# Two hybrid layers with experts on one core: adaLN weights in pairs of chunks, small operations on other engines, stores of experts' results without an order among them

## The chip, the cores and the metric

The kernel runs on one core of one Trainium2 chip. The metric is the time of one execution on the device, in microseconds (us). Three runs of the kernel before gave a median of 2566.57 us (2566.03 to 2566.64).

## The reference

The reference computes two layers of a backbone over 256 context tokens and 512 latent tokens of width 1024, all in float32. In outline, for one layer:

```python
mod = silu(c) @ w_ada + b_ada              # six vectors of 1024 for latents, six for context
h = ln(x) * (1 + scale) + shift
z = h @ w_in                               # one projection for three groups of heads
m = concat(diff_attention(z), mlstm(z), gla(z))
x = ln(ALPHA * x + gate * (m @ w_out)) * g + b
h = ln(x) * (1 + scale2) + shift2
y = sum over a token's 2 experts of weight * (silu(h @ w1[e]) * (h @ w3[e])) @ w2[e]
x = ln(ALPHA * x + gate2 * y) * g2 + b2
```

There are 32 experts in 4 groups with a hidden width of 512; a router picks one group and two experts in it for each token.

## The kernel before, in words

All work runs in the class `Net`. Each operation goes through the helper at L224, so every row of the profile has that line, and groups are told apart by the names of their tiles (out<-in). Two things set the order. `Sched` (L131) keeps a clock for each engine and, among several generators (`Thread`), goes on with the one whose operands are ready first; a generator may yield a time before which it is not to go on. What it writes is then ordered once more by the framework, which plans each engine's queue by a timeline of its own (L2228) and puts in the waits between operations that touch the same tile or tensor. Each engine works through its queue in that order.

A run goes through: the start (0 to 65 us), the mixers of layer 0 (to about 700), its routing (to 760), its experts (to 1322), the passage to layer 1 (to 1470), the mixers of layer 1 (to 1920), routing (to 1970), experts (to 2512) and the end.

`ada` (L557) computes `mod`. `w_ada` is taken in 48 chunks of 128 columns for each layer. A load brings one chunk, `wa` (at the start in tiles borrowed from `hT`), of 128 partitions by 8 by 128. Eight matmuls in four groups of 32 PSUM partitions take the four sums side by side (each is recorded as two), ACT copies PSUM to `adar`, PE transposes it, and `turn` (L567) adds the four sums and the bias `pa` on DVE. 16 chunks run at the start; 32 of layer 0 and 16 of layer 1 are strewn over the mixers of layer 0, 32 over those of layer 1, with `ADA_GAP` (L34) as the distance between them. Two chunks are loaded ahead. `h_open` (L599) opens a layer: it makes these generators, and POOL zeroes `WA` (L623), into which two loads put small gate weights. `u_mlqk` (L819) zeroes three columns of `stg` on POOL for each of four blocks.

`route` (L1673) picks experts and makes the matrices from which `slots` (L1760) computes for each expert block ("slot", up to 128 tokens; 33 in layer 0, 34 in layer 1): `ti` (rows to gather), `di` (rows to store to) and `wt` (weights). `st_slots` (L1865) then has POOL gather `xg` by an indirect DMA. `moe` (L2094) zeroes the three `xg` tiles on DVE first, ahead of the routing.

`run_visits` (L1997) goes through the experts. For wide slots `wsplit` (L1846) splits a piece of weights, 128 by 1024, into `whi` (ACT) and `wlo` = weight - `whi` (DVE or POOL). For the first visit `lo_pool` is 4 (L1597), so that all four pieces of `w1` go to POOL. Narrow slots use the weights unsplit (`part_up`, `part_act`, `part_down`; 32 or 64 columns of PE for each part). The results `ys` are stored to `ybuf` in DRAM by an indirect DMA on POOL (L1947 and L1993). Slots of one layer write other rows of `ybuf`, but to the framework each store writes the whole tensor, so it puts a wait for the former store's landing ahead of each. `part_down` takes `ys` from the two buffers that the wide slots use as well. `final_phase` (L2124) opens the next layer, loads the layer's rows of `ybuf` (L2154) and adds two rows for each token on PE (`big<-whi` or `big<-y`).

Of the kernel before, what the change touches and what calls it, by code (L numbers as in the profile page):

```python
# [7 lines left out]
F32 = mybir.dt.float32  # L8
# [9 lines left out]
D = 1024  # L18
KD = 8
# [32 lines left out]
def host_consts():  # L52
# [12 lines left out]
    def group(g):  # L65
        state["g"] = g
        off[g] = (state["n"], 0)
# [11 lines left out]
    for d in range(2):  # L79
        a, b = (s, l) if d == 0 else (l, s)  # L80
        ms = [(s // 8 == l // 8) & (a <= b)]
        for w in (8, 16, 32):
            ms.append((s // (2 * w) == l // (2 * w)) & (a // w % 2 == 0) & (b // w % 2 == 1))
        group(f"gm{d}")
        for n, m in enumerate(ms):
            add(f"gm{d}{n}", (m & same).reshape(128, 128))
    group("ml")
    add("mh", (p // 64)[:, None] == np.arange(2)[None, :])
    add("negf", np.where(p[:, None] <= p[None, :], 0.0, NEG))
# [159 lines left out]
class Net:  # L249
# [243 lines left out]
    def par0(self, pool):  # L493

        nc, I = self.nc, self.I
        pr = pool.tile([128, 128], F32, name="prow", bufs=1)
        nc.gpsimd.memset(pr, 0.0)
        nc.sync.dma_start(pr[48:56], I["c"][0].rearrange("(b p) -> b p", p=128))
        nc.sync.dma_start(pr[56:64], I["c_ctx"].rearrange("(b p) -> b p", p=128))
        nc.sync.dma_start(pr[0:48], I["b_ada"][0].rearrange("(r p) -> r p", p=128))  # L500
        nc.sync.dma_start(pr[64:112], I["b_ada"][1].rearrange("(r p) -> r p", p=128))
        ps = self.tp.tile([128, 512], F32, name="tp")
        nc.tensor.transpose(ps[:, :128], pr, self.ident)
        self.pa = self.const.tile([128, 128], F32, name="pa")
        nc.vector.tensor_copy(self.pa, ps[:, :128])
        e = self.sm.tile([128, 16], F32, name="ce", bufs=1)
        nc.scalar.activation(e, self.pa[:, 48:64], AF.Exp, scale=-1.0)
        nc.vector.tensor_scalar_add(e, e, 1.0)
        nc.vector.reciprocal(e, e)
        self.cs = self.const.tile([128, KD, 32], F32, name="cs")  # L510
        nc.gpsimd.memset(self.cs, 0.0)
        for m in range(2):
            nc.vector.tensor_mul(self.cs[:, :, m], self.pa[:, 48 + 8 * m:56 + 8 * m], e[:, 8 * m:8 * m + 8])
# [42 lines left out]

    def ada(self, pool, work, nb, gap=0.0, free=()):  # L557

        nc, I = self.nc, self.I
        chunks = [(l, ch) for l, cs in work for ch in cs]  # L560
        ws, free = {}, list(free)

        def load(x):
            w = ws[x] = free.pop(0) if free else pool.tile([128, KD, 128], F32, name="wa")
            nc.sync.dma_start(w, I["w_ada"][x[0]].rearrange("(k p) n -> p k n", p=128)[:, :, x[1] * 128:x[1] * 128 + 128])

        def turn(x, r):  # L567
            layer, ch = x
            t = self.tp.tile([128, 512], F32, name="tp")
            nc.tensor.transpose(t[:, :128], r, self.ident)  # L570
            o = self.mods[layer][:, ch, :]
            nc.vector.tensor_reduce(o, t[:, :128].rearrange("p (g m) -> p m g", g=4)[:, 0:2], axis=AX.X, op=OP.add)
            b = 64 * layer + ch
            nc.vector.tensor_scalar(o, o, self.pa[:, b:b + 1], 1.0 if ch // 8 in (1, 4) else 0.0, op0=OP.add, op1=OP.add)
            self.sch.mark(f"ada{layer}_{ch}")

        for ch in chunks[:nb]:
            load(ch)
        pend = None
        for x, ch in enumerate(chunks):  # L580
            w = ws.pop(ch)

            yield (w, self.sch.clk["tensor"] + gap)
            ps = self.mm.tile([128, 512], F32, name="mm")
            for j in range(2):
                for g in range(4):
                    nc.tensor.matmul(ps[32 * g:32 * g + 32, :128], self.cs[:, 2 * g + j, :], w[:, 2 * g + j, :],
                                     start=j == 0, stop=j == 1)
            r = self.sm.tile([128, 128], F32, name="adar", bufs=2)
            nc.scalar.activation(r, ps[:, :128], AF.Copy)  # L590
            if x + nb < len(chunks):
                load(chunks[x + nb])
            if pend:
                turn(*pend)
            pend = (ch, r)
        yield (pend[1],)
        turn(*pend)

    def h_open(self):  # L599
# [12 lines left out]
        work = ((self.i, range(16, 48)),) + (((1, range(16)),) if self.i + 1 < self.layers else ())  # L612
        self.ta = Thread(self.ada(self.pool(self.S_h, "adap", 2, self.A), work, 2, ADA_GAP[self.i]))
# [16 lines left out]
    def start(self, st):  # L630
# [3 lines left out]
        adap = self.pool(st, "adap0", 4, self.B)  # L634
        self.gar = xp

        free = [x.bitcast(F32).rearrange("p k n -> p (k n)")[:, o:o + 1024].rearrange("p (k n) -> p k n", k=KD)
                for x in self.first for o in range(0, KD * NT, 1024)]
        xs = []

# [5 lines left out]

        for t in range(TT):
            load(t)
        ta = Thread(self.ada(adap, ((0, [x + 8 * y for x in range(8) for y in range(2)]),), 16, free=free))
        ta.step()  # L650
        for x in xs:
            mv, r = self.stats(x)
# [55 lines left out]
    def projections(self):  # L708
# [1213 lines left out]
    def st_down(self, mp, its, ws):  # L1922
# [13 lines left out]
        for it in its:  # L1936
            y = mp.tile([128, D], F32, name="ys")
            m = it.n
            for h in range(2):
# [7 lines left out]
            nc.gpsimd.indirect_dma_start(out=self.ybuf[:, :],  # L1947
                                         out_offset=bass.IndirectOffsetOnAxis(ap=it.di[:m, :1], axis=0),
                                         in_=y[:m], in_offset=None, bounds_check=2 * NT - 1, oob_is_err=False)

    def part_up(self, it, ws):

# [26 lines left out]
    def part_down(self, mp, it, ws):  # L1979
# [13 lines left out]
        nc.gpsimd.indirect_dma_start(out=self.ybuf.rearrange("r (h c) -> (r h) c", h=r),  # L1993
                                     out_offset=bass.IndirectOffsetOnAxis(ap=it.di[:, :1], axis=0),
                                     in_=y, in_offset=None, bounds_check=2 * r * NT - 1, oob_is_err=False)

    def run_visits(self, mp, visits, mid=None):  # L1997

# [20 lines left out]
        for j in range(len(visits) + 1):  # L2019
            if j < len(visits):  # L2020
# [73 lines left out]
    def moe(self):  # L2094
        tc, nc, I, i = self.tc, self.nc, self.I, self.i
        self.ereg = {}
        self.nx = 0
# [26 lines left out]
    def final_phase(self):  # L2124
# [7 lines left out]
        with ExitStack() as st:  # L2132
# [22 lines left out]
            nxt = [[load(free.pop(0), self.ybuf[rows(t, o), :]) for o in (0, NT)] + [x] for t, x in zip(tiles, xs)]  # L2155
# [76 lines left out]
```

## Time and profile before

| | |
|---|---|
| median of 3 runs | 2566.57 us |
| the profiled execution | 2560.8 us, span 2559.0 us |
| busy, share of the span | PE 86%, weight loads 63%, DVE 56%, ACT 34%, POOL 26% |
| mean granted clock of PE | 0.914 |
| moved by DMA | 583.43 MB, mean 228 GB/s |
| matmuls' and loads' instructions | 14811 each |

PE, PEld, DVE, ACT, POOL and SP are the engines (TensorE's matmuls, its weight loads, VectorE, ScalarE, GpSimd and SyncE); SP issues the plain loads, POOL the indirect ones. In a row of a timeline stand start, duration, engine, operation, out<-in with the shape, the number of joined instructions and, in brackets, the engine's idle time before it and what ended that. A stretch of idle time of an engine costs only if the end waits for it.

### The profile page before, as it was taken

The page shows a single profiled execution, that of the slowest core. Times are in us where ns is not written, and L with a number is a line of the kernel's source. Part 1 is how long each engine was busy: PE and PEld are TensorE (multiplying, and loading weights), DVE is VectorE, ACT ScalarE, POOL GpSimd, SP SyncE. Part 2 cuts the span into 40 slices and gives each one's busy share as a digit, 9 for nine tenths or more (in the row PEclk, how much of TensorE's full clock was granted, in tenths as well). Part 3 has the DMA queues.
Part 4 walks back from the last instruction along what each step waited for, and adds up shares of the span by engine and source line. Part 5 has one row for each costly group of instructions (what it writes and reads, how often), then busy time and mean ns, then how long its engine had stood idle before and what let it go on. Part 6 is the DMA issues. An engine that isn't in the chain of part 4 may idle for free. (4 is left out here: it accounts for less than half of the span.)

```text
span 2559.0 us, 39336 instructions
## 1 busy us (share of the span) xinstructions
PE 2192.1 (86%) x14811; PEld 1623.5 (63%) x14811; DVE 1428.6 (56%) x2889; ACT 876.0 (34%) x1589; POOL 661.2 (26%) x537
## 2 busy tenths in 40 slices
PE   5899999978949999999956699989895999889894
PEld 3687888867846656455523488989674667555441
DVE  4566748376886445455408466665778644344313
ACT  2633212265114344444303634112622423233311
POOL 1232322110124233333312223421113322222211
PEclk9899999989969999999986789999996989889997
DMA  9253442321258889999986453313225978999995
GB/s 246 85 150 99 135 139 84 112 62 48 91 207 329 347 316 393 390 366 394 362 324 206 141 157 100 104 34 112 58 85 206 376 313 331 399 414 405 368 395 234
DMA packets 257754, 583.43 MB, mean 228 GB/s; under 512 B 47221, under 2 KB 187621, under 8 KB 208409
## 3 DMA queue, kind: packets, MB, share of 16 engines
q1 hardware_dynamic: 245368, 559.86, 59.9%
q0 software_dynamic: 12192, 21.01, 2.3%
q8 instruction: 119, 1.95, 0.3%
q14 instruction: 75, 0.61, 0.1%
HBM read 553.02 MB, written 46.27 MB: 234 GB/s over the span
## 5 line engine op out<-in xcount | busy, mean ns | idle before, releaser
L224 PE MATMUL mm<-whi,hT 128*128 128x256 f32 (+2 forms) x2144 | 482.9, 317 | 11.2 <-ACT st L224 3.8
L224 DVE TENSOR_TENSOR wlo<-wr,whi 128x1024 fp32r<-128x1024 f32 x217 | 320.8, 1498 | 132.6 <-ACT whi L224 131.6
L224 PEld LDWEIGHTS mm<-whi,hT 128*128 128x128 f32 (+1 forms) x2144 | 363.4, 199 | 40.4 <-issue 6.3
L224 POOL TENSOR_TENSOR wlo<-wr,whi 128x1024 fp32r<-128x1024 f32 x99 | 248.3, 2512 | 522.6 <-ACT whi L224 282.4
L224 ACT ACTIVATE whi<-wr 128x1024 fp32r<-128x1024 f32 x316 | 321.5, 1053 | 164.0 <-PE mm L224 83.3
L224 PE MATMUL mm<-wlo,hT 128*128 128x256 f32 (+2 forms) x1072 | 336.3, 314 | 6.6 <-POOL wlo L224 4.5
L224 PE MATMUL big<-whi,xT 128*128 128x512 f32 (+1 forms) x800 | 264.2, 406 | 4.4 <-ACT xT L224 4.0
L224 PE MATMUL big<-wr,xT 128*32 128x512 f32 (+1 forms) x1344 | 248.6, 613 | 6.9 <-DMA wr<-in_moe_w_dram 3.9
L224 PEld LDWEIGHTS mm<-wlo,hT 128*128 128x128 f32 (+1 forms) x1072 | 212.7, 198 | 23.2 <-POOL wlo L224 8.1
L224 PEld LDWEIGHTS big<-whi,xT 128*128 128x128 f32 (+1 forms) x800 | 146.6, 187 | 44.3 <-ACT xT L224 5.7
L224 POOL DMA_INDIRECT xg<-fdram,ti x67 | 86.1, 1285 | 326.1 <-DVE ti L224 274.8
L224 PE MATMUL big<-wlo,xT 128*128 128x512 f32 (+1 forms) x400 | 162.5, 406 | 1.2 <-DVE wlo L224 1.2
L224 PEld LDWEIGHTS big<-wr,xT 128*32 128x32 f32 (+1 forms) x1344 | 69.6, 126 | 143.5 <-issue 128.1
L224 PE MATMUL mm<-wr,hT 128*32 128x256 f32 (+1 forms) x1008 | 145.5, 515 | 6.1 <-DMA wr<-in_moe_w_dram 3.2
L224 PE MATMUL tp<-cst_base,xg 32*128 32x32 f32 (+3 forms) x536 | 80.8, 288 | 61.5 <-DVE wt L224 39.5
L224 PEld LDWEIGHTS tp<-cst_base,xg 32*128 32x128 f32 (+3 forms) x536 | 70.3, 198 | 91.3 <-DVE wt L224 45.5
L224 ACT ACTIVATE xT<-tp 128x512 fp32r<-128x512 f32 (+3 forms) x92 | 49.0, 532 | 227.4 <-PE tp L224 203.2
L224 PE MATMUL mm<-hT,whi 128*128 128x512 f32 (+3 forms) x400 | 112.6, 370 | 5.0 <-ACT whi L224 4.9
L224 DVE SCALAR_TENSOR_TENSOR hT<-hT,tp 128x128 f32<-128x128 f32 (+1 forms) x84 | 29.6, 353 | 153.9 <-ACT hT L224 151.8
L224 PE MATMUL mm<-wo,mT 128*128 128x512 f32 x480 | 115.4, 397 | 0.0
L224 POOL DMA_INDIRECT ybuf<-ys,di x67 | 74.7, 1115 | 111.6 <-DVE ys L224 33.1
L224 PEld LDWEIGHTS mm<-wo,mT 128*128 128x128 f32 x480 | 88.9, 188 | 19.6
(390 smaller groups left out, 3804.9 us busy)
## 6 DMA issues: line engine op xcount, KB each, us to landing
wr<-in_moe_w_dram SPq DMA_DIRECT2D x384, 1024.0 KB
wa<-in_w_ada_dram SPq DMA_DIRECT2D x84, 512.0 KB
wr<-in_w_in_dram SPq DMA_DIRECT2D x52, 512.0 KB
hT<-in_w_ada_dram SPq DMA_DIRECT2D x12, 512.0 KB
wor<-in_w_out_dram SPq DMA_DIRECT2D x12, 512.0 KB
xmid<-px SPq DMA_DIRECT2D x10, 512.0 KB
fdram<-mT SPq DMA_DIRECT2D x10, 512.0 KB
x<-xmid SPq DMA_DIRECT2D x10, 512.0 KB
```

What stands on the lines that cost most here:

```text
L224: r = f(*a, **kw)
```

## The change

- A: `ada` takes pairs of chunks, 256 columns at a time. Two loads bring a pair, each half the rows at 256 columns. Eight matmuls of 256 columns, one `adar` of 256 columns (one buffer), two transposes and two DVE operations serve two chunks. The 1 of `1 + scale` is added to `pa` beforehand. The next pair is loaded after the matmuls of this one, and the gap between pairs is twice as long.
- B: the zeros of `WA` come by two loads. C: the columns of `stg` are zeroed on DVE.
- D: the `xg` tiles are zeroed by ACT (0 times the identity).
- E: the four `wlo` of the first visit go to DVE, with a factor `one` that is computed from the second slot's `wt`, so after the routing.
- F: stores of one layer are declared free of one another. `part_down` has `ys` buffers of its own, two or four.
- G: the loads of `ybuf` in the last phase wait for each store of the layer.

```diff
@@ par0
+        for o in (8, 32):
+            v = self.pa.rearrange("p (l c) -> p l c", l=2)[:, :, o:o + 8]
+            nc.vector.tensor_scalar_add(v, v, 1.0)
@@ ada
-        chunks = [(l, ch) for l, cs in work for ch in cs]
-            w = ws[x] = free.pop(0) if free else pool.tile([128, KD, 128], F32, name="wa")
-            nc.sync.dma_start(w, I["w_ada"][x[0]].rearrange("(k p) n -> p k n", p=128)[:, :, x[1] * 128:x[1] * 128 + 128])
+        pairs = [(l, p) for l, ps in work for p in ps]
+        tiles = [(l, p, h) for l, p in pairs for h in range(2)]
+                w = ws[x] = free.pop(0) if free else pool.tile([128, 4, 256], F32, name="wa")
+                nc.sync.dma_start(w, I["w_ada"][l].rearrange("(k p) n -> p k n", p=128)[:, 4 * h:4 * h + 4, p * 256:p * 256 + 256])
...
-            nc.tensor.transpose(t[:, :128], r, self.ident)
+            for c in range(2):
+                nc.tensor.transpose(t[:, 128 * c:128 * c + 128], r[:, 128 * c:128 * c + 128], self.ident)
...
-            nc.vector.tensor_scalar(o, o, self.pa[:, b:b + 1], 1.0 if ch // 8 in (1, 4) else 0.0, op0=OP.add, op1=OP.add)
+            nc.vector.tensor_tensor(o, o, self.pa[:, b:b + 2, None].to_broadcast([128, 2, 2]), op=OP.add)
...
-                    nc.tensor.matmul(ps[32 * g:32 * g + 32, :128], self.cs[:, 2 * g + j, :], w[:, 2 * g + j, :],
-                                     start=j == 0, stop=j == 1)
-            r = self.sm.tile([128, 128], F32, name="adar", bufs=2)
-            nc.scalar.activation(r, ps[:, :128], AF.Copy)
-            if x + nb < len(chunks):
-                load(chunks[x + nb])
+                    nc.tensor.matmul(ps[32 * g:32 * g + 32, :256], self.cs[:, 4 * h + g, :], w[h][:, g, :],
+                                     start=h == 0, stop=h == 1)
...
+            r = pool.tile([128, 256], F32, name="adar", bufs=1)
+            nc.scalar.activation(r, ps[:, :256], AF.Copy)
+            load(nb + 2 * x + 2)
@@ h_open
-        self.nc.gpsimd.memset(self.WA, 0.0)
...
+            self.nc.sync.dma_start(self.WA[16 * d:16 * d + 16, 1 - d, :], self.I["cst"][0:16, o:o + 128])
@@ u_mlqk
-                for z in (0, 257, 770):
-                    nc.gpsimd.memset(raw[:, z:z + 1], 0.0)
...
+                    for z in (0, 257, 770) if t0 == part[0][0] else ():
+                        nc.vector.tensor_scalar(raw[:, z:z + 1], ps[:, 0:1], 0.0, 0.0, op0=OP.min, op1=OP.max)
@@ wsplit
-        (nc.gpsimd if pool_lo else nc.vector).tensor_tensor(lo, src, hi.bitcast(F32), op=OP.subtract)
+        if pool_lo and self.one is not None:
+            nc.vector.scalar_tensor_tensor(lo, src, self.one, hi.bitcast(F32), op0=OP.mult, op1=OP.subtract)
+        else:
+            (nc.gpsimd if pool_lo else nc.vector).tensor_tensor(lo, src, hi.bitcast(F32), op=OP.subtract)
@@ st_slots
+            if self.nx == 1:
+                self.one = self.sm.tile([128, 1], F32, name="one", bufs=1)
+                nc.vector.tensor_scalar(self.one, it.wt, -1.0, None, op0=OP.is_gt)
@@ part_down (in st_down the store is wrapped the same way)
-        y = mp.tile([128, D], F32, name="ys")[:, 0:n]
+        y = mp.tile([128, n], F32, name=f"ys{r}", bufs=r)
...
+        self.stored(nc.gpsimd.indirect_dma_start(
...
+    def stored(self, ins):
+        for x in self.stores:
+            self.tc.declare_no_dep(ins.ins, x, reason="rows of other slots")
+        self.stores.append(ins.ins)
@@ run_visits
-                self.lo_pool = 0
+                self.lo_pool, self.one = 0, None
@@ moe
-            nc.vector.memset(x, 0.0)
+            nc.scalar.activation(x.rearrange("p (a b) -> p a b", b=128), self.ident[:, None, :].to_broadcast([128, 8, 128]),
+                                 AF.Copy, scale=0.0)
@@ final_phase
+            def loady(y, src):
+                ins = nc.sync.dma_start(y, src)
+                for x in self.stores:
+                    self.tc.add_manual_dep(ins.ins, x.name, mybir.DependencyInfo(
+                        mybir.DependencyClass.Sync, mybir.DependencyReason.DATA), reason="rows of all slots")
+                return y
```

## Rows read from the trace of the kernel before

**Rows 1.** Busy time by stretch: length, PE, PEld, DVE, ACT, POOL, clock, DMA share, GB/s

```profile
768.00:1310.00 542.00, 505.76 (x2533) 305.05 (x2531) 265.56 (x355) 221.18 (x287) 173.98 (x99) 0.96 0.94 365
1984.00:2512.00 528.00, 480.11 (x2661) 291.82 (x2659) 210.10 (x339) 155.85 (x210) 139.11 (x89) 0.94 0.94 376
15.00:35.00 20.00, 14.94 (x170) 8.14 (x170) 9.10 (x33) 2.77 (x10) 2.32 (x3) 1.00 1.21 291
```

**Rows 2.** Instructions of the tile adar (ns min/median/max), and who waited for them

```profile
L224 ACT ACTIVATE adar<-mm x96: 253/277/321, 17.0 to 1553.8; 128x128 f32<-128x128 f32 x96
...
  PEld mm L224: 22.6, 20
```

**Rows 3.** Timeline of PE: a chunk of ada, and 16 records of 256 columns

```profile
1364.87 0.65 PE L224 MATMUL mm<-wa,cs 128*32 128x128 f32 x16 [1.28 <-DMA wa<-in_w_ada_dram]
...
2507.37 1.07 PE L224 MATMUL mm<-wr,hT 128*32 128x256 f32 x16 [0.97 <-DMA wr<-in_moe_w_dram]
```

**Rows 4.** Timeline of the routing of layer 0

```profile
726.71 0.15 DVE L224 TENSOR_TENSOR eg<-eg,mn 128x4 f32<-128x4 f32 x1
...
731.66 3.90 ACT L224 ACTIVATE whi<-wr 128x1024 fp32r<-128x1024 f32 x4 [2.28 <-PE mm L224]
...
732.02 0.91 DVE L224 MEMSET xg<- 128x1024 f32 x1 [0.16 <-issue]
...
732.79 9.25 POOL L224 TENSOR_TENSOR wlo<-wr,whi 128x1024 fp32r<-128x1024 f32 x4 [0.37 <-ACT whi L224]
...
735.13 2.41 DVE L224 TENSOR_TENSOR eg<-lg,rv 128x4 f32<-128x4 f32 x2
737.50 2.26 DVE L224 SCALAR_TENSOR_TENSOR eg<-eg,cst_rt 128x4 f32<-128x4 f32 x1
737.57 0.21 ACT L224 ACTIVATE eg<-eg 128x4 f32<-128x4 f32 x1 [2.02 <-DVE eg L224]
...
739.99 2.07 DVE L224 TENSOR_TENSOR eg<-eg,mn 128x4 f32<-128x4 f32 x1
...
745.33 0.50 PE L224 MATMUL tp<-cA,cnt 128*128 128x192 f32 x1 [13.70 <-DVE rv L224]
```

**Rows 5.** Waits of PE in the expert stages of layers 0 and 1: us, times, longest

```profile
PE tp L224 <- DVE wt L224: 12.9, 7, 2.3
...
PE tp L224 <- DVE wt L224: 26.6, 10, 6.0
```

**Rows 6.** The tile ybuf: who waited for it, and its DMAs from issue to landing

```profile
  DVE di L224: 1.9, 1
...
DMA to landing us min/median/max: 2.0/7.7/10.8
```

**Rows 7.** Timeline of the end of layer 0's experts

```profile
1319.93 0.98 POOL L224 DMA_INDIRECT ybuf<-ys,di  x1 [0.46 <-issue]
...
1326.51 0.48 DVE L224 TENSOR_SCALAR ys<-mm,wt 128x256 f32<-128x256 f32 x1 [9.69 <-DMA ybuf<-ys,di]
...
1336.78 0.97 POOL L224 DMA_INDIRECT ybuf<-ys,di  x1 [2.06 <-issue]
...
1342.20 3.02 PE L224 MATMUL tp<-cst_base,mod 128*128 128x128 f32 x12 [20.55 <-issue]
```

**Rows 8.** The chain that ended last (start, us, what), and PE's row of the timeline

```profile
2512.00 6.66 DMA ybuf<-ys,di
...
2519.74 2.73 DMA ybuf<-ys,di
...
2527.24 15.46 PE L224 MATMUL big<-y,cst_base 128*128 128x512 f32 x32 [15.55 <-DMA y<-ybuf]
```

**Rows 9.** Timeline of POOL, and DMA issues of 2010 to 2030 us (KB, us to landing)

```profile
2027.06 1.19 POOL L224 DMA_INDIRECT xg<-fdram,ti  x1 [8.98 <-DVE ti L224]
2028.56 1.01 POOL L224 DMA_INDIRECT ybuf<-ys,di  x1 [0.30 <-issue]
...
ybuf<-ys,di POOLq DMA_INDIRECT x2, 8.3
```

More of the change, by code (lines that the diff above doesn't have):

```diff
@@ L86, in host_consts @@
             add(f"gm{d}{n}", (m & same).reshape(128, 128))
+    group("zero")
+    add("z128", np.zeros(128))
     group("ml")
@@ L559, in ada @@
         nc, I = self.nc, self.I
[L560 to L565 removed]
+        pairs = [(l, p) for l, ps in work for p in ps]
+        tiles = [(l, p, h) for l, p in pairs for h in range(2)]
+        ws, free, ld = {}, list(free), 0
@@ L567, in turn, with load @@
+        def load(upto):
+            nonlocal ld
+            while ld < min(upto, len(tiles)):
+                l, p, h = x = tiles[ld]
+                ld += 1
+                w = ws[x] = free.pop(0) if free else pool.tile([128, 4, 256], F32, name="wa")
+                nc.sync.dma_start(w, I["w_ada"][l].rearrange("(k p) n -> p k n", p=128)[:, 4 * h:4 * h + 4, p * 256:p * 256 + 256])
         def turn(x, r):
-            layer, ch = x
+            layer, p = x
             t = self.tp.tile([128, 512], F32, name="tp")
-            nc.tensor.transpose(t[:, :128], r, self.ident)
@@ L579, in ada @@
+            o = self.mods[layer][:, 2 * p:2 * p + 2, :]
+            nc.vector.tensor_reduce(o, t[:, :256].rearrange("p (c g m) -> p c m g", c=2, g=4)[:, :, 0:2], axis=AX.X, op=OP.add)
+            b = 64 * layer + 2 * p
+            nc.vector.tensor_tensor(o, o, self.pa[:, b:b + 2, None].to_broadcast([128, 2, 2]), op=OP.add)
+        load(nb)
         pend = None
-        for x, ch in enumerate(chunks):
-            w = ws.pop(ch)
-            yield (w, self.sch.clk["tensor"] + gap)
+        for x, (l, p) in enumerate(pairs):
+            w = [ws.pop((l, p, h)) for h in range(2)]
+            yield tuple(w) + (self.sch.clk["tensor"] + gap,)
@@ L584, in ada @@
             ps = self.mm.tile([128, 512], F32, name="mm")
-            for j in range(2):
+            for h in range(2):
                 for g in range(4):
-                    nc.tensor.matmul(ps[32 * g:32 * g + 32, :128], self.cs[:, 2 * g + j, :], w[:, 2 * g + j, :],
-                                     start=j == 0, stop=j == 1)
-            r = self.sm.tile([128, 128], F32, name="adar", bufs=2)
-            nc.scalar.activation(r, ps[:, :128], AF.Copy)
-            if x + nb < len(chunks):
-                load(chunks[x + nb])
+                    nc.tensor.matmul(ps[32 * g:32 * g + 32, :256], self.cs[:, 4 * h + g, :], w[h][:, g, :],
+                                     start=h == 0, stop=h == 1)
@@ L610, in h_open @@
         self.rc = self.pool(self.S_h, "rc", 1, self.A)
-        work = ((self.i, range(16, 48)),) + (((1, range(16)),) if self.i + 1 < self.layers else ())
-        self.ta = Thread(self.ada(self.pool(self.S_h, "adap", 2, self.A), work, 2, ADA_GAP[self.i]))
+        work = ((self.i, range(8, 24)),) + (((1, range(8)),) if self.i + 1 < self.layers else ())
+        self.ta = Thread(self.ada(self.pool(self.S_h, "adap", 2, self.A), work, 2, 2.0 * ADA_GAP[self.i]))
         self.S_g = ExitStack()
@@ L622, in h_open @@
         self.WA = T("WA", [32, 2, 128])
-        self.nc.gpsimd.memset(self.WA, 0.0)
+        o, _ = self.off["zero"]
         for d in range(2):
+            self.nc.sync.dma_start(self.WA[16 * d:16 * d + 16, 1 - d, :], self.I["cst"][0:16, o:o + 128])
             self.nc.sync.dma_start(self.WA[16 * d:16 * d + 16, d, :], self.I["gl_wa"][self.i, d])
@@ L635, in start @@
         self.gar = xp
-        free = [x.bitcast(F32).rearrange("p k n -> p (k n)")[:, o:o + 1024].rearrange("p (k n) -> p k n", k=KD)
+        free = [x.bitcast(F32).rearrange("p k n -> p (k n)")[:, o:o + 1024].rearrange("p (k n) -> p k n", k=4)
                 for x in self.first for o in range(0, KD * NT, 1024)]
@@ L648, in start @@
             load(t)
-        ta = Thread(self.ada(adap, ((0, [x + 8 * y for x in range(8) for y in range(2)]),), 16, free=free))
+        ta = Thread(self.ada(adap, ((0, [x + 4 * y for x in range(4) for y in range(2)]),), 16, free=free))
         ta.step()
@@ L1946, in st_down @@
                     nc.gpsimd.tensor_tensor(y[:m, hs], y[:m, hs], self.g2[0][:m, hs], op=OP.mult)
-            nc.gpsimd.indirect_dma_start(out=self.ybuf[:, :],
-                                         out_offset=bass.IndirectOffsetOnAxis(ap=it.di[:m, :1], axis=0),
-                                         in_=y[:m], in_offset=None, bounds_check=2 * NT - 1, oob_is_err=False)
+            self.stored(nc.gpsimd.indirect_dma_start(
+                out=self.ybuf[:, :], out_offset=bass.IndirectOffsetOnAxis(ap=it.di[:m, :1], axis=0),
+                in_=y[:m], in_offset=None, bounds_check=2 * NT - 1, oob_is_err=False))
     def part_up(self, it, ws):
@@ L1992, in part_down @@
             nc.vector.tensor_scalar(y, py[:, :n], it.wt, None, op0=OP.mult)
-        nc.gpsimd.indirect_dma_start(out=self.ybuf.rearrange("r (h c) -> (r h) c", h=r),
-                                     out_offset=bass.IndirectOffsetOnAxis(ap=it.di[:, :1], axis=0),
-                                     in_=y, in_offset=None, bounds_check=2 * r * NT - 1, oob_is_err=False)
+        self.stored(nc.gpsimd.indirect_dma_start(
+            out=self.ybuf.rearrange("r (h c) -> (r h) c", h=r),
+            out_offset=bass.IndirectOffsetOnAxis(ap=it.di[:, :1], axis=0),
+            in_=y, in_offset=None, bounds_check=2 * r * NT - 1, oob_is_err=False))
+    def stored(self, ins):
+        for x in self.stores:
+            self.tc.declare_no_dep(ins.ins, x, reason="rows of other slots")
+        self.stores.append(ins.ins)
     def run_visits(self, mp, visits, mid=None):
@@ L2096, in moe @@
         self.ereg = {}
-        self.nx = 0
+        self.nx, self.one, self.stores = 0, None, []
         rp, mp = self.rpm, self.mow
@@ L2154, in final_phase @@
             xs = [load(finx.tile([128, D], F32, name=f"x{t}"), self.xmid[rows(t), :]) for t in tiles]
-            nxt = [[load(free.pop(0), self.ybuf[rows(t, o), :]) for o in (0, NT)] + [x] for t, x in zip(tiles, xs)]
+            def loady(y, src):
[4 more added lines that the diff above has]
+                return y
+            nxt = [[loady(free.pop(0), self.ybuf[rows(t, o), :]) for o in (0, NT)] + [x] for t, x in zip(tiles, xs)]
             g2 = {} if self.g2 else {m: self.modrow(5, m, f"g2{m}") for m in ms}
```

8 lines of the change are left out of this document (1 added, 7 removed).

## Prediction, made before the change was run

> **What bounds it.** I read the busy time by stretch first, then the waits inside the stretches, then timelines around each edited line. In both expert stages (542 and 528 us of the 2559 us span) PE is busy 505.76 and 480.11 us and the DMA engines show a share of 0.94 at 365 and 376 GB/s [rows 1]: there the time belongs to PE and to the weight stream almost equally, and 36 and 48 us are left in which PE does nothing. The rest of PE's idle time lies between stages: while a routing is computed, while the last results are stored and read back, and at the start. The change works on those seams, and on PE's own work in the small matmuls of `ada`. So I price seams one by one; each lies on the path if PE's gap there ends on the edited thing.
>
> **Part A, ada in pairs.** 96 chunks become 48 pairs; the 96 copies `adar` give the count [rows 2]. One chunk's 16 matmul records of 128 columns took 0.65 us at full clock; 16 records of 256 columns took 1.07 us in the form that a pair will have [rows 3]. Two chunks are 1.30, one pair is 1.07: 0.23 us saved. 16 chunks lie in the start and wait for their loads anyway, so 40 pairs count: 40 x 0.23 = 9; I take -8.5 us, since a few run beside a wait. The 96 transposes stay. On DVE, ACT and SP (still 96 loads of 512 KB, now with rows twice as long) the edit only takes away or leaves equal. Loads of matmul weights waited 22.6 us, 20 times, for `adar` copies [rows 2]; half as many copies should take part of that away, but a pair holds a PSUM buffer for longer and the copy has one buffer: between +3 and -10, I take -3. At the start 16 chunks of 512 KB arrive at 291 GB/s [rows 1], 29 us; at the stream's rate in the expert stages (376 at a share of 0.94, so 400) they would need 21. Between 0 and -8; the rows of the loads only double, to 1 KB, so I take -3.
>
> **Parts B and C, memsets off POOL.** Small work in any case: WA is 32 partitions by 256 and a margin of `stg` one column. Two more small loads stand in SP's queue beside the gate weights, and 24 tiny operations join DVE ahead of copies that wait for the same matmuls of PE: I take 0, the cover being that PE has other matmuls to go on with; without it each costs at most one such small step on DVE, 0.16 us [rows 4], 4 us in all. What the POOL memsets do to the stores behind them is counted with F.
>
> **Parts D and E, the routing.** In layer 0 DVE zeroes `xg` three times at 0.91 us before the routing's own operations. Then POOL subtracts four pieces of `wlo` for 9.25 us, and in that time three steps of the routing on DVE on 4 columns take 2.41 (two operations), 2.26 and 2.07 us, where the same subtraction took 0.15 a little earlier [rows 4]. PE waits 13.70 us for the end of this chain [rows 4]. Removed from the chain: 3 x 0.91 with their issue gaps, 3 us, and 2.41 + 2.26 + 2.07 - 4 x 0.16 = 6.1 us, together 9. What is late next is ACT: four casts of `whi` occupy it for 3.90 us from 731.66, and the Exp that the chain needs stands behind them at 737.57 [rows 4]. Three zeroings more on ACT, at about one of these casts each (3.90/4 = 1 us), can stand ahead of it too. With Exp after casts and zeroings (731.66 + 3.9 + 3 = 738.6) it would start 1 us later than now and only what comes after it (2.26 + 2.07, less normal price) is saved: -3. With Exp first of all, the whole -9. I take the middle, -5.5, in each layer, as layer 1 shows the same four pieces and the same slow operations: -11 (-5 to -18). The four `wlo` on DVE are ordered behind the second slot's weights, so while the first gather is in flight; at no more than POOL's price they need 9.25 us [rows 4], and a transfer of POOL's queue takes 7.7 [rows 6] before PE starts on the slot: covered, or up to 1.5 us late per layer, which the middle allows for.
>
> **Part F and G in the slots.** 67 slots store in turn, each store waiting until the former one has landed: 7.7 us median, 2.0 to 10.8 [rows 6]. The wait seldom reaches PE. PE's gaps that end on a slot's `wt`, computed behind `di` whose buffer such a store frees, are 12.9 us in stage 0 and 26.6 in stage 1 [rows 5]: that is the most there is, -39.5. Against it: the issue order on POOL stays, with the next gather ahead of a ready store, and a part of the gaps has its `ys` only just finished; and where the weight stream runs at its limit, PE would only catch up with it. I take a tenth, -4 (0 to -20).
>
> **The tails.** In layer 0 the last stores are chained: POOL's store at 1319.93, a `ys` that waited 9.69 us on DVE for a store to free its buffer, the last store at 1336.78, and PE idle 20.55 us until 1342.20 [rows 7]. Its last result but for that chain is ready shortly after PE's last matmul, 20.55 us before 1342.20, so 1321.65. With one buffer more per slot and no order the last `ys` ends at 1322.5, its store goes by 1324, as three follow one another at 1 us of POOL each, and lands with the median 7.7 us at 1331 against 1339 or a little more now: -8 (-3 if landings stretch, -14 if they take 2 us). In layer 1 the last two stores are at 2512.00 with 6.66 us and 2519.74 with 2.73 us, then the reads, and PE waits 15.55 us until 2527.24 [rows 8]. The second would go at 2513.2 and land 6.66 us later at 2519.9 instead of 2522.5: -2.6 (0 to -7). Sum of tails -10.5. The Trainium skill, DMA: Bandwidth & Descriptors, section "Anatomy of one DMA — SWDGE (gpsimd) path", fits 2.0 us plus the bytes at 436 GB/s, about 2.3 for one of these stores; the trace agrees only with its quickest landing, 2.0 [rows 6], and the median of 7.7 speaks against it while loads stream. By that page the last stores would land at 1326.3 and 2515.5, and the two tails would give -20.
>
> **Sum.** -8.5 - 3 - 3 - 11 - 4 - 10.5 = -40. The profiled run took 2560.8 us, so 2520.8 for it; the median of the runs shown, 2566.57, is 5.8 above it, so 2526 for a median run.
>
> **Rivals.** (1) *DVE blocks on di.* Without the chain a store no longer holds POOL, so the schedule may put `di` of a later slot earlier on DVE, where it waits for the landing of the store that frees its buffer, with `wlo` pieces behind it and PE behind those. Price: if a third of the 67 slots waits 4 us of a 7.7 us landing, 22 x 4 = +88, less the 40 won: +48, 2615; it ends slower from about 10 such waits. Against: DVE waited only 1.9 us in all for a store with `di` [rows 6], and stores now leave earlier, not later. 0.06. (2) *The weight stream takes it back.* In stages with a DMA share of 0.94 [rows 1] an earlier first slot only means an earlier wait for weights; routing and slots (-15) vanish, and what is left is -25: 2541. For it: 365 and 376 GB/s over whole stages. Against: 0.06 of 542 and 528 us is 32 and 32 us of slack, more than is won. 0.17. (3) *The stores still go one by one.* If the queue serves one transfer at a time, the wait moves from POOL into the queue: landings stay in turn, slots and tails (-14.5) vanish: 2541. The Trainium skill, same page, section "SWDGE vs HWDGE vs iDMA", says that only one such queue is allocated. Against: a gather issued at 2027.06 and a store at 2028.56 were both in flight, and stores of that stretch landed after 8.3 us all the same [rows 9]. 0.10. (4) *Pairs starve.* A pair's two tiles are requested only when the matmuls of the pair before are done, and 1 MB must then land in one gap; PE already waited 1.28 us on `wa` for a single chunk at the layer change [rows 3]. If 10 of 40 pairs wait 1.3 us more, +13: 2539. 0.12. My own case, between 2505 and 2535, has 0.50; 0.05 is for a schedule that comes out differently enough to leave the time about where it was.
>
> **How the numbers follow.** About 0.2% (5 us) is what a measurement of this kernel can tell from no change: below 2561.4 is faster, above 2571.7 slower. Faster holds my case and rivals 2, 3 and 4 (0.89), same the 0.05, slower rival 1 (0.06). All lower bounds together are -8.5 - 10 - 8 - 18 - 20 - 21 = -86; I let the range go down to -70, 2496. At the top it takes in rivals 2 to 4 and two of them together, -40 + 15 + 13 = -12, and with the upper bound of the routing instead of the middle -6, so 2560.
>
> **What would show it.** Right: `ada` records of 128x256 form in half the number; routing steps of 0.2 us on DVE and no 2 us ones, PE's gap after the router shorter by 3 to 9; stores issued about 1 us apart in the tails with overlapping landings; layer 0's gap down from 20.55 to about 12, layer 1's from 15.55 to about 13. Wrong: DVE waits for `ybuf` of tens of us (rival 1), PE waits for `wr` growing in the expert stages by what routing won (2), the last landings in the tails still 6 us apart (3), PE waits for `wa` above 10 us (4). A shift of the whole schedule, since every instruction's place is planned anew, would show as other gaps moving in stages that the edits do not touch.

## The result, and the profile after

The changed kernel took 2508.41 us (median of 4 runs), the kernel before 2566.3 us beside it: 0.9781 of it, 95% interval 0.9766 to 0.9797, or -56 us. In the experiments (changed_again) it was 0.9806 (0.9777 to 0.9835), -50 us. Forecast were 2526 us and a range of 2496 to 2560. So the time lay in the range and the sign was right. The sum was 16 us short, and its terms were wrong in both directions. One execution of stores_only, 3188 us at a granted clock of 0.635, is left out of its ratio; its other nine took 2532 to 2555 us at 0.917 to 0.928.

I cut both profiled executions at the same events on PE: the first and last matmul of a stage. The steps of the difference (after minus before) are then: start -4.7 us; mixers of layer 0 -8.1; routing -6.0; experts of layer 0 -0.3; the tail after them +0.7; opening and mixers of layer 1 -11.5; routing -7.1; experts of layer 1 -15.6; last tail -0.3. The experts' stages of the kernel before, cut like that (first `big<-whi,xT` to the last `mm<-wr,hT`; columns as in [rows 1]):

```profile
762.12:1321.65 559.53, 520.97 (x2635) 314.42 (x2634) 269.92 (x364) 224.78 (x292) 175.45 (x107) 0.96 0.93 362
1973.25:2511.69 538.44, 490.86 (x2705) 300.81 (x2704) 216.94 (x349) 161.52 (x216) 143.09 (x91) 0.93 0.92 370
```

and of the changed kernel:

```profile
743.41:1302.67 559.26, 533.49 (x2635) 315.92 (x2634) 275.94 (x362) 224.36 (x292) 179.23 (x102) 0.96 0.94 363
1936.39:2459.24 522.85, 486.75 (x2705) 296.69 (x2704) 226.41 (x349) 160.40 (x216) 143.81 (x92) 0.96 0.95 381
```

In the first stage the length stays to 0.3 us although PE has 12.8 us less idle time (38.6 and 25.8); in the second 15.6 us go and the granted clock is 0.96 instead of 0.93. Against full clock that is 0.07 of 538 us and 0.04 of 523 us, 38 and 21 us (an estimate from these rows), which is as much as the stage got shorter. Over all profiles here the kernels with ordered stores have a granted clock of 0.93 to 0.95 in that stage, those with free stores 0.95 to 0.97; that the clock rose because waits went is not shown. The wait that the stores were to shorten, `tp` for `wt` [rows 5], is gone from both stages. What leads PE's waits in the second one now (from 1937 to 2460 us):

```profile
PE tp L226 <- ACT hs L226: 10.3, 13, 1.1
PE big L226 <- DVE wlo L226: 5.9, 5, 1.6
```

Stores still land after several us, as far as the trace has it (8 of 67 landings; 61 of 67 before), and nothing but the last sums waits for them. The tile `ybuf` after, answering to [rows 6]:

```profile
who waited for it (us, times):
  PE big L226: 22.1, 2
  PEld big L226: 17.3, 3
...
DMA to landing us min/median/max: 3.7/6.7/8.2
```

The tile `adar` after, answering to [rows 2]:

```profile
L226 ACT ACTIVATE adar<-mm x48: 362/383/419, 18.9 to 1512.9; 128x256 f32<-128x256 f32 x48
...
  PEld mm L226: 2.6, 2
```

Half as many copies, and the 22.6 us that weight loads of `mm` waited for them are 2.6. That is not all time of PE: PE's own waits for `adar` went from 13.8 to 3.2 us, and the weight loads of the transposes waited 11.9 us for it instead of 5.5. The routing of layer 0 after, answering to [rows 4] (timeline):

```profile
719.19 2.95 ACT L226 ACTIVATE xg<-cst_base 128x1024 f32<-128x1024 f32 x3 [2.28 <-PE mm L226]
...
719.61 0.23 DVE L226 TENSOR_TENSOR eg<-lg,rv 128x4 f32<-128x4 f32 x2
...
722.04 3.88 ACT L226 ACTIVATE whi<-wr 128x1024 fp32r<-128x1024 f32 x4
...
723.62 0.50 PE L226 MATMUL tp<-cA,cnt 128*128 128x192 f32 x1 [4.47 <-DVE V L226]
...
725.83 0.19 ACT L226 ACTIVATE eg<-eg 128x4 f32<-128x4 f32 x1
...
734.24 2.28 POOL L226 DMA_INDIRECT xg<-fdram,ti  x1 [14.29 <-DVE wt L226]
735.59 4.88 DVE L226 SCALAR_TENSOR_TENSOR wlo<-wr,one,whi 128x1024 fp32r<-128x1024 f32 x4
...
736.83 5.06 POOL L226 DMA_INDIRECT xg<-fdram,ti  x1 [0.31 <-issue]
```

The two operations that took 2.41 us take 0.23, and PE's wait is 4.47 instead of 13.70. But Exp stands behind three zeroings and four casts on ACT, and `wt` needs it, so 9.2 us won up to PE's 723.62 are 6.0 at the first expert matmul. PE's 723.62 itself does not need Exp, which starts 2.2 us later. The second gather's issue took 5.06 us beside the four `wlo` on DVE, but 1.01 us beside the same four in another run of this kernel (changed_again) and in routing_only, so it is no lasting price of E. The Trainium skill, SBUF — State Buffer, section "SBUF: two separate sides", states an exclusive lock between DVE operations with two inputs from SBUF and POOL operations that read SBUF, held for a whole instruction; the 2.07 to 2.41 us of [rows 4], beside POOL operations of 2.3 us each, and the 0.23 here, with none beside it, agree.

The tail after layer 0, answering to [rows 7] (timeline, then the loop's line; a q after an engine is its sequencer):

```profile
1302.74 0.48 DVE L226 TENSOR_SCALAR ys<-mm,wt 128x256 f32<-128x256 f32 x1 [2.33 <-PE mm L226]
...
1315.92 3.87 PE L226 MATMUL tp<-cst_base,mod 128*128 128x128 f32 x16 [13.25 <-issue]
...
1316.43 0.97 POOL L226 DMA_INDIRECT ybuf<-ys,di  x1 [14.77 <-issue]
...
1323.46 1.84 SPq L226 DMA_DIRECT2D whi<-ybuf  x4
...
1327.20 8.84 PE L226 MATMUL big<-whi,cst_base 128*128 128x512 f32 x16 [6.79 <-DMA whi<-ybuf]
```

```profile
L2148 POOLq COMPARE_BRANCH  x3: 37/38/54, 1301.3 to 1315.5; - x3
...
L2148 POOLq INC_SWDGE_SEM  x1: 1481/1481/1481, 1308.4 to 1308.4; - x1
L2148 ACTq COMPARE_BRANCH  x1: 37/37/37, 1315.7 to 1315.7; - x1
```

The last `ys` is ready at 1303.22, its store is issued at 1316.43. In between POOL goes through L2148, a loop over experts with more tokens than their slots hold (`moe`, at L2120 in the kernel before). It runs zero times here, and still stops every engine: POOL takes its first branch at 1301.3, and ACT, the last to leave, at 1315.7. SP's waits in that time show what the loop stands still for, transfers that are in flight (1290 to 1330 us):

```profile
SPq L2148 <- DMA ybuf<-ys,di: 5.4, 1, 5.4
SPq L2148 <- DMA x<-xmid: 4.7, 1, 4.7
```

In the kernel before the loop comes after the last store and takes 4.7 us from POOL's first branch, 1337.5 to 1342.2. Freed from its order, the last store was planned behind this loop. The loads of `ybuf`, which G ties to that store, follow 7.0 us after its issue, at 1323.46. Ahead of them SP issues fifteen other loads for the next layer, one right after another from 1315.43 to 1323.42, and the landing of this store is not in the trace; so it is not shown which of the two held the loads of `ybuf`.

### The profile page after: what moved, and what is told of

The parts are those of the page before. It is cut to its first block, busy times and chain, and to the rows that moved or that the text cites. A ratio compares the mean times of both kernels' runs of the same rounds, so it can differ in the third digit from the quotient of the medians.

```text
span 2506.5 us, 37612 instructions
## 1 busy us (share of the span) xinstructions
PE 2176.8 (87%) x14043; PEld 1584.9 (63%) x14043; DVE 1426.6 (57%) x2830; ACT 870.4 (35%) x1542; POOL 646.7 (26%) x501
## 5 line engine op out<-in xcount | busy, mean ns | idle before, releaser
L226 PEld LDWEIGHTS mm<-whi,hT 128*128 128x128 f32 (+1 forms) x2144 | 361.4, 198 | 41.7 <-issue 10.3
L226 POOL TENSOR_TENSOR wlo<-wr,whi 128x1024 fp32r<-128x1024 f32 x93 | 235.6, 2535 | 365.4 <-ACT whi L226 226.7
L226 PE MATMUL big<-wr,xT 128*32 128x512 f32 (+1 forms) x1344 | 265.3, 612 | 4.5 <-DMA wr<-in_moe_w_dram 4.5
L226 PE MATMUL mm<-wr,hT 128*32 128x256 f32 (+1 forms) x1008 | 134.7, 498 | 1.5 <-DMA wr<-in_moe_w_dram 1.5
L226 POOL DMA_INDIRECT xg<-fdram,ti x67 | 92.1, 1375 | 154.1 <-DVE ti L226 104.8
L226 PEld LDWEIGHTS big<-wlo,xT 128*128 128x128 f32 (+1 forms) x400 | 74.6, 186 | 39.4 <-DVE wlo L226 15.3
```

The source lines that it names most:

```text
L226: r = f(*a, **kw)
```

## Experiments

Each is compared with the kernel before on its own chip; us are worked out from ratios of runs there (before: 2559 to 2563). Three chips served: one for stores_only, stores_undone, routing_only and ada_only, a second for changed_again, loop_store_ordered, fewer_bytes and xg_on_pool, a third for the other four. Stage lengths come from one profiled execution each, and for stages whose code is the same they scatter by 5 us and more together with the granted clock (0.96 to 0.99 in the experts of layer 0).

**stores_only**: the kernel before with the lines of F and G. **stores_undone**, and again as **stores_ordered_again**: the changed kernel without them.

```diff
@@ stores_undone, stores_ordered_again (st_down, part_down, final_phase)
-            self.stored(nc.gpsimd.indirect_dma_start(
+            nc.gpsimd.indirect_dma_start(
...
-        y = mp.tile([128, n], F32, name=f"ys{r}", bufs=r)
+        y = mp.tile([128, D], F32, name="ys")[:, 0:n]
...
-            nxt = [[loady(free.pop(0), self.ybuf[rows(t, o), :]) for o in (0, NT)] + [x] for t, x in zip(tiles, xs)]
+            nxt = [[load(free.pop(0), self.ybuf[rows(t, o), :]) for o in (0, NT)] + [x] for t, x in zip(tiles, xs)]
```

> The kernel before with parts F and G alone (stores free of one another, part_down's own ys buffers, loads of ybuf waiting for all stores). Theory 1 (the experts' stage of layer 1 got its 15.6 us from the stores, since all of PE's 26.6 us of waits for a slot's wt went away, while in stage 0 the weight stream took the 12.9 us back): -15 us, about 2551, nearly all of it in the experts of layer 1, none of it in the two tails, where the last store again stands behind the overflow loop on POOL and PE's gap stays near 20 us. Theory 2 (stage 1 was quicker because it was planned anew and began earlier, the stores have little to do with it): 0 to -4 us, 2563 to 2566, with 20 us or more of wt waits left in stage 1.

> The changed kernel without F and G: stores ordered as before, one pair of ys buffers for all. Theory 1: loses what stores gave, 2508 + 15 = 2523 us; PE's waits for wt in stage 1 are back at 20 us or more; the tails are as long as before (PE's gap 20 us after layer 0, 15.5 after layer 1), so that these neither win nor lose. Theory 2: 2508 to 2512 us. If the tails do depend on the order of the stores, this kernel's last store stands ahead of the loop on POOL, as before.

> The changed kernel without F and G once more, beside the kernel with the loop's store in order. Theory 1 (free stores are worth some 10 us in the experts' stages, 36 us of waits for wt gone and most of it taken back, and cost 2 to 4 us in the tails where the last store fell behind the loop): 2512 to 2518 us, that is 14 to 20 us above loop_store_again. Theory 2 (free stores give nothing in the experts' stages, everything is taken back): 2500 to 2508, less than 8 above loop_store_again, and that only from the tails.

Measured: alone 0.9937 (0.9912 to 0.9962), -16 us, with experts' stages of 551.2 and 528.9 us and the last store after layer 0 again behind the loop. Undone 0.9816 (0.9782 to 0.9851) and 0.9795 (0.9775 to 0.9815), where the changed kernel has 0.9806 on another chip and 0.9781 in the first measurement. So in this change the stores give nothing that can be measured, against theory 1, which gave them 15 us both ways. Beside loop_store_again, on one chip, stores_ordered_again is 15.7 us slower (2511.51 and 2495.81), as its own theory 1 had it. The mechanism of the stores is there in any case. PE's waits with stores in order (stores_ordered_again, stages 0 and 1) and its stages:

```profile
PE tp L226 <- DVE wt L226: 12.9, 7, 2.3
...
PE tp L226 <- DVE wt L226: 23.5, 8, 6.6
```

```profile
740.28:1301.14 560.86, 521.13 (x2635) 318.28 (x2634) 270.13 (x362) 225.02 (x292) 176.94 (x101) 0.96 0.93 362
1926.30:2458.40 532.10, 488.69 (x2705) 298.96 (x2704) 219.30 (x349) 161.07 (x216) 140.58 (x92) 0.94 0.94 374
```

The stages with ordered stores took 557.4 and 560.9, 532.6 and 532.1 us. With free stores and both routing edits they took 555.8, 556.0 and 550.5, and 523.0, 529.4 and 531.3 (the changed kernel and the two runs of loop_store below). The means differ by 5 and 4.5 us: some 10 us of the 36 us of waits. Over all seven profiles with free stores and D and E the first stage took 550.5 to 561.7 us and the second 522.6 to 531.3 (fewer_bytes left aside), so ordered stores lie outside the scatter only in the second, and there by little. The tail after layer 0 took 20.1 and 19.0 us with ordered stores and 22.5 and 24.5 in the changed kernel: 4 us given back. The mixers of layer 1 took 518.7 and 523.9 us in the changed kernel and 509.2 and 513.4 with ordered stores, which takes back the rest. This is not the stores' doing: xg_on_pool and fewer_bytes (below) have free stores and their last store behind the loop as well, and took 513.9 and 514.1; ada_only took 514.2. PE's sequence of operations in that stretch, told by the names of the tiles, is alike to 99% in these kernels and that of loop_store_ordered, and only to 96% between them and the changed kernel. The changed kernel alone got another plan there, 5 to 15 us longer.

**loop_store_ordered**, and again as **loop_store_again**: only the store inside the loop keeps its order after the others.

```diff
-        for x in self.stores:
+        for x in self.stores if it.over is None else ():
             self.tc.declare_no_dep(ins.ins, x, reason="rows of other slots")
```

> The changed kernel, but the store inside the overflow loop (which runs zero times here) keeps its order after the stores ahead of it, so that the last store of a layer must stand ahead of the loop on POOL; all other stores stay free. Theory 1 (the last store, whose ys is ready 13 us earlier, waited on POOL behind the loop that stops all engines, and the loads of ybuf waited for it): the last store is issued within 1 us of its ys, the loads of ybuf follow the loop at once; PE's wait before the first sum of ybuf rows gets 7 us shorter after layer 0 and 3 us after layer 1: -10, about 2498 us. Theory 2 (the loop itself, or the loads of x that land at 1314.7, sets when work goes on, whatever the last store does): 0 to -3 us.

> The changed kernel with the loop's store in order, again, as the partner of the other three: 0.975 of the kernel before, 2495 to 2500 us.

0.9751 (0.9725 to 0.9776) and 0.9742 (0.9723 to 0.9761): 2497.93 and 2495.81 us. On the same chips that is 12 us below changed_again and 16 below stores_ordered_again, 14 and 14 by the ratios. The timeline of the tail (loop_store_ordered):

```profile
1297.33 0.48 DVE L226 TENSOR_SCALAR ys<-mm,wt 128x256 f32<-128x256 f32 x1 [3.96 <-PE mm L226]
...
1298.09 0.97 POOL L226 DMA_INDIRECT ybuf<-ys,di  x1 [3.47 <-DVE ys L226]
...
1310.57 1.84 SPq L226 DMA_DIRECT2D whi<-ybuf  x4
...
1314.33 1.12 PE L226 MATMUL big<-whi,cst_base 128*128 128x512 f32 x2 [1.58 <-DMA whi<-ybuf]
```

The store leaves 0.3 us after its `ys`, and the loads of `ybuf` follow the loop, now ahead of most of SP's other loads. The tails took 17.1 and 18.6 us (after layer 0) and 13.3 and 13.0, against 22.5 and 14.5 in the changed kernel's run there: -6. So theory 1 holds, with 6 of its 10 us in the tails. The rest lies mostly in the mixers of layer 1, 512.3 and 511.0 us against 523.9 (518.7 in the first profile); there the plan orders PE's matmuls otherwise and the clock is 0.94 instead of 0.93. Since xg_on_pool and fewer_bytes have that plan with the last store behind the loop, this part belongs to the plan and not to the loop's store. Why that plan is better was not tried.

**fewer_bytes**: narrow slots load half of `w2`.

```diff
-        ws = self.load_e(its[0], "moe_w2")
+        ws = self.load_e(its[0], "moe_w2", (0,)) * 2 if its[0].parts > 1 else self.load_e(its[0], "moe_w2")
```

> The changed kernel, but narrow slots (19 experts in layer 0, 23 in layer 1) load only the first half of w2 and use it for both halves: 19 and 23 MB less of 201 MB for each layer, with PE's work unchanged; results of these experts leave out the second half of w2. Theory 1 (in stage 0 the weight stream took back what the free stores gave: PE is slowed by weights that land late): stage 0 gets 10 to 25 us shorter, stage 1 5 to 20, in all -15 to -45. Theory 2 (PE with its granted clock sets the length of both stages, and the waits moved to other places of PE's own chain): within 5 us of the changed kernel in both stages together.

0.9672 (0.9641 to 0.9703), 31 to 34 us below the changed kernel on the same chip; some 10 of these are the mixers of layer 1 with the other plan. Its stages:

```profile
742.34:1285.12 542.78, 523.85 (x2635) 313.54 (x2634) 276.42 (x362) 223.64 (x292) 179.70 (x102) 0.98 0.89 336
1913.78:2424.65 510.87, 483.11 (x2705) 297.39 (x2704) 224.45 (x349) 159.35 (x216) 146.24 (x92) 0.97 0.88 342
```

Both are 12 to 13 us shorter than in changed_again (555.8 and 523.0) with PE's instructions unchanged: theory 1. The weight stream does slow PE in these stages, and can take back what a wait gave. It is not the only bound: 42 MB less, some 115 us at 366 GB/s, bought 25 us in the two stages.

**routing_only**: the kernel before with the lines of D and E (`wsplit`, `st_slots`, `run_visits`, `moe` in the diff of the change). **xg_on_pool**: the changed kernel with `xg` zeroed on POOL. **changed_again**: the changed kernel as their partner.

```diff
@@ xg_on_pool
-            nc.scalar.activation(x.rearrange("p (a b) -> p a b", b=128), self.ident[:, None, :].to_broadcast([128, 8, 128]),
-                                 AF.Copy, scale=0.0)
+            nc.gpsimd.memset(x, 0.0)
```

> The kernel before with parts D and E alone (xg zeroed on ACT, the first four wlo on DVE after the routing). Theory 1 (steps add): -6.2 us at the routing of layer 0 and -7.4 at that of layer 1, 2553 us; the three DVE steps of 2.1 to 2.4 us take 0.2, and ACT's three zeroings stand ahead of Exp. Rival (the weight stream takes back what an earlier first slot wins): the gap at the router shrinks by the same 6 to 7 us, but the experts' stages grow by as much and the time stays within 4 us of 2566.

> The changed kernel with the three xg tiles zeroed by POOL instead of ACT. Theory 1 (the routing now waits for ACT: Exp stands behind three zeroings, 2.95 us, and four casts, 3.88 us): Exp starts 2.9 us earlier in each layer, the first gather is issued some 2.5 us earlier, -5 in all, about 2503 us. Theory 2 (the chain through DVE sets the gather, Exp has room): within 1 us of the changed kernel; if POOL's zeroing slows DVE as its subtractions did, DVE's small steps take 1 us and more again and the time is 2 to 4 us longer.

> The changed kernel itself, so that the three that differ from it by one edit are compared with it on one chip. About 0.979 of the kernel before, 2506 us, with the steps by stage of its first profile except where the granted clock differs.

routing_only: 0.9898 (0.9871 to 0.9926), -26 us. Of that the routings hold 14.6 against ada_only on the same chip (41.5 and 39.9 us against 48.0 and 48.0). The rival falls, and the remaining 4 to 18 us are in no stage by more than its scatter. xg_on_pool: 0.9800 (0.9774 to 0.9826). Its routing of layer 0:

```profile
715.69 3.90 ACT L226 ACTIVATE whi<-wr 128x1024 fp32r<-128x1024 f32 x4 [2.27 <-PE mm L226]
719.49 0.19 ACT L226 ACTIVATE eg<-eg 128x4 f32<-128x4 f32 x1
...
727.49 1.29 POOL L226 DMA_INDIRECT xg<-fdram,ti  x1 [8.36 <-DVE wt L226]
```

Exp starts 3.80 us after the casts could begin, instead of 6.64, and the routings are 2.8 and 2.4 us shorter, as theory 1 had it. The time does not show it: the ratio is that of the changed kernel, though 5 us less would lie in its interval too.

**loop_store_xg_pool** joins the two edits; **exp_ahead_of_casts** also ties the four casts to the second slot's `wt`.

```diff
@@ exp_ahead_of_casts
-        nc.scalar.activation(hi, src, AF.Copy)
+        if pool_lo and self.one is not None:
+            nc.scalar.activation(hi, src, AF.Copy, scale=self.one)
+        else:
+            nc.scalar.activation(hi, src, AF.Copy)
```

> The loop's store in order and xg zeroed on POOL. Theory 1 (gains at the routers last to the end): the routings of both layers 5.2 us shorter together and the time 4 to 6 us below loop_store_again. Theory 2 (the experts' stages end when the weight stream ends, and that does not begin sooner): the routings are 5 us shorter, the experts' stages longer by about as much, and the time within 2 us of loop_store_again.

> As the kernel with the loop's store in order and xg zeroed on POOL, but the four casts of the first visit are tied to the second slot's wt like their wlo, so that Exp stands ahead of them on ACT. Theory 1: the first gather of each layer goes 2 to 3 us earlier still and the time is 3 to 6 us below loop_store_xg_pool, unless the casts come late for the first matmuls, then 0. Theory 2 (weight stream): the gap after the router is shorter by the same, the time within 2 us of loop_store_xg_pool.

0.9726 (0.9707 to 0.9744), 2491.01 us, 4.8 below its partner; and 0.9716 (0.9699 to 0.9732), 2490.49 us. Intervals overlap, so the step from loop_store_again is likely, not shown. The last one won nothing: Exp starts 2.97 us after its engine fell idle, as soon as DVE has its operand, yet the products that give `ti` come no earlier after the router's matmuls: 723.98 - 714.64 = 9.34 us here, 727.23 - 717.88 = 9.35 in loop_store_xg_pool. Exp was no longer what is late. The timeline of exp_ahead_of_casts:

```profile
711.01 3.63 PE L226 MATMUL mm<-gw,mT 128*128 128x36 f32 x16
...
715.36 0.20 ACT L226 ACTIVATE eg<-eg 128x4 f32<-128x4 f32 x1 [2.97 <-DVE eg L226]
...
723.98 2.69 PE L226 MATMUL tp<-V,wr 128*128 128x4 f32 x12 [3.48 <-issue]
```

and of loop_store_xg_pool:

```profile
714.25 3.63 PE L226 MATMUL mm<-gw,mT 128*128 128x36 f32 x16
...
727.23 2.69 PE L226 MATMUL tp<-V,wr 128*128 128x4 f32 x12 [3.48 <-issue]
```

**ada_only**: the kernel before with the lines of A (`par0`, `ada` and the lists of pairs).

> The kernel before with part A alone (pairs of chunks). Theory 1: start -4.7, mixers of layer 0 -7.9, passage and mixers of layer 1 -11 us: -24, about 2542 us. Rival (part of the mixers' gain is the memsets taken off POOL, or the new plan, and not the pairs): 40 pairs at 0.23 us and the start alone, -9 - 4.7 = -14, about 2552.

0.9901 (0.9878 to 0.9924), -25 us: theory 1. PE's groups by shape (count, busy us, mean ns), of the kernel before:

```profile
L224 PE MATMUL mm<-wa,cs 128*32 128x128 f32 x1344 | 62.3, 306 | 23.9 <-DMA wa<-in_w_ada_dram 12.5 <-ACT adar L224 9.8 <-ACT glk L224 1.1
L224 PE MATMUL tp<-cst_base,adar 128*128 128x128 f32 x96 | 34.3, 357 | 16.3 <-ACT htmp L224 6.8 <-DVE mod L224 3.4 <-ACT adar L224 2.3
```

and of ada_only:

```profile
L224 PE MATMUL mm<-wa,cs 128*32 128x256 f32 x672 | 53.4, 417 | 20.7 <-DMA wa<-in_w_ada_dram 17.2 <-ACT stg L224 1.9 <-ACT st L224 1.6
L224 PE MATMUL tp<-cst_base,adar 128*128 128x128 f32 x96 | 22.5, 317 | 11.7 <-ACT htmp L224 8.0 <-ACT adar L224 3.5 <-DVE pcl L224 0.3
```

The busy time of the matmuls falls by 8.9 us, that of the transposes, the same 96, by 11.8. Such a sum counts time in which other operations of PE ran beside them. Timelines of PE, a lone transpose in the kernel before and a pair in ada_only:

```profile
94.12 0.33 PE L224 MATMUL tp<-cst_base,adar 128*128 128x128 f32 x1
94.21 0.71 PE L224 MATMUL mm<-hT,whi 128*128 128x512 f32 x2
...
94.49 0.44 PE L224 MATMUL tp<-cst_base,adar 128*128 128x128 f32 x2
```

The next matmul begins 0.09 us after the lone transpose, which is busy for 0.33. Counted over the mixers of both layers, the time that PE was busy with nothing but these matmuls and transposes fell from 60.8 to 54.3 us, by 6.5; the time that other operations filled fell by 10.3, and the mixers by 18.4. What made the others shorter is not shown; the granted clock of layer 1's mixers is 0.93 instead of 0.92. Waits for `wa` rise by 4.7.

## Why the prediction was right and where it failed

- **ada** (-14.5 forecast, -25 measured). By busy time the matmuls' term was right: -8.5, and 8.9 measured. The step that failed is that the sum ended with `ada`'s own operations and the waits for them: of the 18.4 us that the mixers got shorter in ada_only, 10.3 lie in other operations of PE, a term that the prediction lacks and whose cause stays open. The transposes that "stay" are busy for 11.8 us less, but mostly in time that others filled as well. The waits for `adar` were under-sized (3 taken; PE's own went from 13.8 to 3.2 in the changed kernel). The start gave 4.7 for 3. Pairs did not starve: PE waited 12.5 us for `wa` before, 17.2 in ada_only and 10.6 in the changed kernel, so the sign "above 10 us" could tell nothing.
- **Routing** (-11, measured -13.1 in the two stages). The number came out by luck. Exp went behind zeroings and casts in full and started 6.68 us after the router's last matmul instead of 5.95, the case that the prediction priced at -3 a layer; the routings still won 6.0 and 7.1. The step that failed is that Exp was put into the chain of PE's 13.70 us: PE's operation at 723.62 stands ahead of Exp, which holds up `wt` and the gather. Exp was what came late next: xg_on_pool took the zeroings from ahead of it and got 5.2 us in the routings.
- **Slots** (-4, 0 to -20). The most there was, 39.5, was right, and the waits went away entirely; some 10 us of them reached the stages. The 15.6 us of layer 1's stage are not all theirs: ada_only and routing_only, with ordered stores, took 530.9 and 533.6 us there, 5 to 8 less than the kernel before. The weight-stream rival can explain part of the difference (fewer_bytes), so it holds inside the experts' stages, though not for the routing as a whole.
- **Tails** (-10.5, measured +0.4). This step failed. It let the last store go "by 1324, as three follow one another at 1 us of POOL each", and never asked what else stands in POOL's queue between the last `ys` and the loads: the loop of L2120, a stop of all engines that costs time even with no pass. In the kernel before the order of the stores kept the last one ahead of the loop; the freedom that should bring it forward let the plan put it behind. The sign "layer 0's gap down from 20.55 to about 12" came true, 13.25, and told nothing: PE then does 4 us of other work and waits 6.79 us more for `ybuf`. With that one order back the two tails take 30.4 and 31.6 us together, against 39.3 in the kernel before: 8 of the 10.5.
- **Rivals.** DVE has no wait for `ybuf` any more, so the first falls. Stores one by one falls too: the waits for `wt` are gone, and in the kernel before a store issued at 2015.46 and a gather at 2017.05 landed 8.3 and 10.2 us later, so both were in flight together. (Of the pair that the prediction names, the store's landing is not in the trace.)
- **Sum.** ada and routing alone give 51 us, A to E together, with B and C, 47 and 52 (the two runs without F and G), and the change 50 to 56. That the forecast landed in its range is in part luck: by the stages of the first two profiles, `ada`'s (start and mixers) gave 10 us and the experts 12 us more than forecast, the tails 11 less. Stores alone gave 16 us and nothing on top of the other parts. The changed kernel has two burdens that the kernel without F and G lacks: some 4 us in the tail, and a plan of its own in the mixers of layer 1, 5 to 15 us longer; together that is about what is missing. Against loop_store_again, which has neither, ordered stores cost 16 us again. Why the planner took that plan is open.

## What to carry to other kernels

When an order between operations is removed, look for what that order also kept in place: an operation that is free to move can land behind a barrier, and a loop that runs zero times is one. Before pricing a seam, list every queue's entries between the two events, the sequencer's own lines too. The busy time of a group also counts what ran beside it; look at what begins next before a price is drawn from it. And when parts of a change do not add up, compare the order of operations in stages that no edit touches: there a new plan alone made 5 to 15 us here.

## What the hardware showed beyond that

- In the changed kernel's two profiled executions the experts' stage of layer 0 moved 363 and 366 GB/s at a DMA share of 0.94 and 0.95, that of layer 1 381 and 382 at 0.95 and 0.96: 3 to 4% more for the same share, with weights of the same size. No run here says why.
- The same program's stage took 556.0 us at a granted clock of 0.97 and 550.5 at 0.99 (loop_store_ordered and loop_store_again, on two chips). A few us in one stage of one profile are not an edit's.
